# A trunk layer on one core: the first feed-forward regrouped from 6, 6, 6, 4 to 8, 8, 6 inner tiles, with the eights' down-projection in seven half products

## The chip, the core and the metric

The kernel runs on one core of a Trainium2 chip. TensorE (PE) multiplies, VectorE (DVE) and ScalarE (ACT) do element-wise work, GpSimd (POOL) and SyncE (SP) mostly start transfers. The metric is device microseconds of one execution; three runs of the kernel before gave 1647.42, 1647.49 and 1647.60 us, so the median is 1647.49 us. Lower is better.

## What is computed

One layer of a hybrid diffusion backbone on 128 context tokens and 512 latent tokens, 640 in all, each of width 1024, in fp32:

```python
mod = silu(cond) @ w_mod + b_mod                     # nine vectors: sh1, sc1, g1, shm, scm, gm, sh2, sc2, g2
h = modulate(rmsnorm(x, norm_g[0]), sh1, sc1)
x = x + 0.5 * g1 * swiglu(h, ffn1_w1, ffn1_w2)       # first feed-forward
h = modulate(rmsnorm(x, norm_g[1]), shm, scm)
y, C, n, m = mixer(h, ...)                           # mLSTM in two directions, short convolution, gates
x = x + gm * y
h = modulate(rmsnorm(x, norm_g[2]), sh2, sc2)
x = x + 0.5 * g2 * swiglu(h, ffn2_w1, ffn2_w2)       # second feed-forward
# swiglu(h, w1, w2): a, b = split(h @ w1); return (silu(a) * b) @ w2,  inner width 2816 = 22 tiles of 128
```

The context tokens have their own modulation vectors. A final RMSNorm and the mLSTM states are outputs too.

## The kernel before

The 640 tokens lie along the free axis in two halves of 320 columns, and every product is made of matmuls of 128x128 weights against 128x320 activations. To keep fp32 accuracy, each operand is split into a rounded high part (an ACT cast, line 75) and the remainder (a DVE subtraction, line 79), and one product is three matmuls (lines 288 to 290). The text calls these "main matmuls".

**Seven products for eight.** Two output tiles of a projection are made together as a "pair" (`pair_el`). Its weights and activations form 2x2 blocks (output tile by half of the contraction, half of the contraction by token half), and a Strassen-like scheme makes seven block products (`ORDER`: A11, S1, S2, A12, S3, S4, A22) where the plain way has eight. Each needs one weight block of 128x512 (some are sums of blocks, made by DVE at line 270, or, if the pair is "summed", by accumulating transfers on POOL's queue) and an activation operand, named 11, 21, 22, T1 to T4. With 8 tiles of contraction a pair has 7 x 4 x 3 = 84 main matmuls, where the plain way (`plain_el`) has 96.

**Feed-forward.** The 22 inner tiles go in groups: up-projection of a group, then its down-projection. The up-projection is in pairs (silu half and linear half of an inner tile), apart from the first tiles, which the "head" makes in the plain way while the modulated input is still being finished. A down-projection over 6 or 4 tiles is plain. In the first feed-forward the groups are 6, 6, 6, 4, and the residual X stays in SBUF, to which `add_x` (line 1017) adds. In the second they are 8, 8, 6: for a group of eight (`eights`) the inner activations are put into the seven operand forms (the sums by DVE), the down-projection is four pairs, the residual lies in DRAM (`xd`), results are added there by POOL's accumulating transfers (line 1030), and the input's forms T3 and T4 are parked in DRAM meanwhile (`h_away`, `h_back`). The last group, of six, is plain and ends in `halves_el`: three weight tiles for the left half of the tokens, then the same for the right half, with the next stage's norm (statistics at line 898, spreading at line 915, scaling, modulation and splitting of the next input) placed between the right half's products. In the group of four there are six such tiles of 12 matmuls.

**Modulation vectors.** The first gate (G1) is made on PE in eight units: 512 KB of w_mod each, two matmuls of 32x512 that occupy a quarter of the array's columns each (line 649). In the kernel before, POOL loads these into a pool of their own (`mg`), and two units are multiplied at one place. SHM, SCM and half of SH2 are made by DVE (`mod_dve`, lines 769 and 771: per unit four passes over 128x512), 20 units spread evenly over the feed-forward, and closed by matmuls with ones (line 780), SHM's two halves at one place and SCM's too.

**Order.** The order of the work on every engine is that in which the Python code emits it; nothing reorders it. Weights come through a ring of five 512 KB buffers (`wr`) on SP's queue, with splits made four operands ahead of the product that uses them.

Of the kernel before, what the change touches and what calls it, by code (L numbers as in the profile page):

```python
# [12 lines left out]
P = 128  # L13
# [31 lines left out]
def mixer_step(ctx: ExitStack, tc: tile.TileContext, x_prompt, x_sample, state_C, state_n, state_m,  # L45
# [503 lines left out]
    st = st_x.enter_context(pool("st"))  # L549
# [159 lines left out]
    def mod_own(ch):  # L709


        us, fs, tiles = [], [], {}
        for half in range(2):
            u, f = mod_half(ch, half, True)
            us += [(mod_load(ch, half, i, G), u[i][1]) for i in range(4)]
            fs.append(f)

        def load(*ii):
            for i in ii:
                tiles[i] = PO["mg"].tile([P, 1024], F32, name="mg", bufs=2)  # L720
                if i < 2:

                    G.tensor_copy(tiles[i][:, 0:1], modT[:, SH1, KT - 1, 0:1])
                us[i][0](tiles[i])

        def two(v, *more):
            def f():
                for i in (2 * v, 2 * v + 1):
                    us[i][1](tiles.pop(i))
                if v < 3:  # L730
                    load(2 * v + 2, 2 * v + 3)
                for m in more:
                    m()
            return f
        none = lambda: None
        return (lambda: load(0, 1),
                [two(0), none, two(1, fs[0][0]), fs[0][1], two(2, fs[0][2]), none, two(3, fs[1][0]), none], fs[1][1:])
# [68 lines left out]
    def with_units(main, units, spare=0):  # L806
# [4 lines left out]
        post = []  # L811
        for i, el in enumerate(main):
            el = dict(el, raws=list(el["raws"]), fill=list(el.get("fill", ())))
            now, post = post[:1], post[1:]
            while e < m and e * n < (i + 1) * m:
# [228 lines left out]
    def eights(w1, w2, g, f0, n_head, head, more, back):  # L1044
# [12 lines left out]
        def put_own(o, k, src):  # L1057
            UB[o][k] = hl = upair()
            split(src, *hl)
# [40 lines left out]
        for j in range(8):  # L1100
# [6 lines left out]
            if due:  # L1107
                pops = {1: (3, 2, 1), 2: (2, 2, 2), 3: (3, 2)}.get(due, (2, 8) if j < 5 else (8,))
                at = joined(at, {i + 1: [lambda n=n: relax_some(n)] for i, n in enumerate(pops)})
            if f0 + j < n_head:  # L1110
                head.extend(blocks_of(p))
            else:
                grp.append(pair_el(*p, at=joined(at, more.get(j, {})), spare_v=j in spare, calm=True,
                                   summed=j > (1 if f0 < n_head else 3)))
        w2s = []
        PO["x_end"] = []
        for m in range(0, KT, 2):
# [17 lines left out]
            elif m == KT - 2 and back:  # L1135
                at = {4: [lambda: h_back("T3")], 6: [lambda: h_back("T4")]}
            w2s.append(pair_el(w_load(w2, f0 * P, 8, m * P, D), w_load(w2, f0 * P, 8, (m + 1) * P, D), ev,
                               acts=UB, at=at, gated=rows_, spare_v=m == 0, summed=m == 0))
        return grp, w2s

    def ffn(w1, w2, g, lists, head_of, n_head, e1=None, groups=(6, 6, 6, 4), more={}):

        head, els, f0 = [], [], 0
        for gi, size in enumerate(groups):
            if size == 8:
                els.append(eights(w1, w2, g, f0, n_head, head, more.get(gi, {}), True))
                f0 += size
                continue
            U = {}
            grp = []  # L1150
            for j in range(size):
# [16 lines left out]
                else:  # L1168
                    grp.append(pair_el(*p, e1 if f0 == 0 else None, at=more.get(gi, {}).get(j)))
# [30 lines left out]
    PO["un"] = 12  # L1200
# [70 lines left out]
    def first_head(blocks):  # L1271
# [22 lines left out]
        def emit():  # L1294
# [74 lines left out]
            for f in lower(1, 6, 7):  # L1369
                f()  # L1370
            close_early()
# [53 lines left out]
    def close_early():  # L1425
        early_x.close()
        PO["hq"] = ctx.enter_context(pool("hq", side="right"))
# [40 lines left out]
    head, els = ffn(ffn1_w1, ffn1_w2, G1, after_lists(1, SHM), first_head, 3)  # L1468
    PO["ma_x"] = ExitStack()
    PO["mg_x"] = ExitStack()  # L1470

    def open_mg():
        PO["mg"] = PO["mg_x"].enter_context(pool("mg"))
    g_first, g_mid, g_last = mod_own(G1)
    prog += [head, step(open_mg), step(g_first)] + weave(els[0][0], [step(f) for f in g_mid])
    els[0][1][0] = dict(els[0][1][0], fill=[step(f) for f in g_last + [half_gate(G1)]])

# [3 lines left out]
    def open_ma():  # L1481
        PO["mg_x"].close()
        PO["ma"] = PO["ma_x"].enter_context(pool("ma"))

    def ma_wide():
        return [PO["ma"].tile([P, 512], F32, name="ma", bufs=4)]

    prog += [step(open_ma), step(gate_weights_)]
    main = []
# [751 lines left out]
```

## Time and profile before

| | us |
|---|---|
| median of 3 runs | 1647.49 |
| the profiled execution's own time | 1648.61 |
| its span, first to last instruction | 1646.8 |
| first feed-forward: head's end, then pairs up to the last plain product | 77.0 to 478.9 |
| second feed-forward: first pair to the last product | 1241.7 to 1646.8 |

The page lists each engine's busy share, groups of instructions, and the chain that ended last. A row of the stretches view reads: stretch, its length, then for each engine the busy time with the number of instructions, the granted TensorE clock, the share of the DMA engines that were busy, and GB/s. A row of the timeline reads: start, length, engine, line, operation, output<-inputs, shape and count; the length of a matmul contains its pipeline, so the distance of starts is what one costs.

### The profile page before, as it was taken

To read this page: it belongs to the slowest core of one execution; us is meant where nothing else is said; L and a number is where in the kernel's file an instruction comes from. 1 tells how busy PE (TensorE), PEld (TensorE's weight loads), DVE (VectorE), ACT (ScalarE), POOL (GpSimd) and SP (SyncE) were. 2 spreads that over 40 slices of the span, in tenths; PEclk is the share of its full clock that TensorE was granted. 3 is DMA by queue.
4 is the path that set the end of the run, shared out by engine and by line. 5 is a ranking of instruction groups with operands and counts; after the bars stand their busy time and mean duration, and the time that the engine had idled before them with its cause. 6 is when DMAs were issued, how large, how long until landed. Compare 5 with 4: busy or idle time off the path is not lost.

```text
span 1646.8 us, 29482 instructions
## 1 busy us (share of the span) xinstructions
PE 1628.1 (99%) x11093; PEld 1585.3 (96%) x11093; DVE 1284.7 (78%) x2714; ACT 837.8 (51%) x1841; POOL 251.9 (15%) x362
## 2 busy tenths in 40 slices
PE   7999999999999999999999999999999999999998
PEld 5989999999999999999999999999999999999997
DVE  6867887887878878787887788879778877786765
ACT  5542542542566656455562455642276665565543
POOL 2010000000031221121121222011133113113002
PEclk9999999999999999999999999999999999999999
DMA  9454343343353443342358333357468768468522
GB/s 321 117 164 120 99 127 114 110 119 100 103 172 101 109 106 87 81 114 70 96 165 270 109 90 90 91 167 222 136 177 179 156 134 197 105 134 199 167 81 65
DMA packets 302607, 220.88 MB, mean 134 GB/s; under 512 B 9844, under 2 KB 279547, under 8 KB 302465
## 3 DMA queue, kind: packets, MB, share of 16 engines
q1 hardware_dynamic: 269680, 161.50, 34.3%
q0 software_dynamic: 32752, 57.49, 14.7%
q8 instruction: 87, 1.43, 0.4%
q14 instruction: 56, 0.45, 0.1%
q10 hardware_dynamic: 32, 0.01, 0.0%
HBM read 193.18 MB, written 25.79 MB: 133 GB/s over the span
## 4 chain that ended last, share of the span: by engine, by line
PE 89%; DVE 4%; ACT 3%; DMA 2%; issue 1%; SPq 1%; POOL 0%; ACTq 0%; DVEq 0%; POOLq 0%
PE ps L288 27%; PE ps L289 27%; PE ps L290 27%; PE ax L1780 2%; PE ax L1811 2%; DMA wr<-in_ffn_w_dram 1%; PE ax L1783 1%; DVE wl L79 1%; PE ax L1757 1%; ACT Uh L931 1%; ACT wh L75 1%; SPq L627 0%; DMA wl<-in_x_sample_dram 0%; DVE Uh L923 0%; PE ax L780 0%
## 5 line engine op out<-in xcount | busy, mean ns | idle before, releaser
L79 DVE TENSOR_TENSOR wl<-wr,wh 128x512 fp32r<-128x512 f32 (+1 forms) x401 | 272.9, 692 | 86.3 <-ACT wh L75 83.9
L75 ACT CAST wh<-wr 128x512 fp32r<-128x512 f32 (+1 forms) x403 | 235.8, 598 | 91.1 <-PE ps L289 71.3
L79 DVE TENSOR_TENSOR wl<-ws,wh 128x512 fp32r<-128x512 f32 x300 | 207.5, 692 | 56.2 <-ACT wh L75 55.6
L75 ACT CAST wh<-ws 128x512 fp32r<-128x512 f32 x300 | 183.7, 620 | 96.9 <-DVE ws L270 68.9
L288 PE MATMUL ps<-Uh,wh 128*128 128x320 f32 x576 | 179.6, 312 | 0.0
L289 PE MATMUL ps<-Ul,wh 128*128 128x320 f32 x576 | 177.9, 309 | 0.0
L290 PE MATMUL ps<-Uh,wl 128*128 128x320 f32 x576 | 177.7, 308 | 0.0
L288 PE MATMUL ps<-HT4h,wh 128*128 128x320 f32 x408 | 128.4, 315 | 0.0
L289 PE MATMUL ps<-HT4l,wh 128*128 128x320 f32 x408 | 126.4, 310 | 0.6 <-DVE HT4l L79 0.5
L290 PE MATMUL ps<-HT4h,wl 128*128 128x320 f32 x408 | 126.1, 309 | 0.0
L288 PE MATMUL ps<-H11h,wh 128*128 128x320 f32 x376 | 118.8, 316 | 0.5 <-ACT H11h L75 0.5
L288 PE MATMUL ps<-H21h,wh 128*128 128x320 f32 x376 | 117.7, 313 | 0.0
L289 PE MATMUL ps<-H11l,wh 128*128 128x320 f32 x376 | 116.5, 310 | 0.3
L290 PE MATMUL ps<-H21h,wl 128*128 128x320 f32 x376 | 116.3, 309 | 0.0
L290 PE MATMUL ps<-H11h,wl 128*128 128x320 f32 x376 | 116.1, 309 | 0.0
L289 PE MATMUL ps<-H21l,wh 128*128 128x320 f32 x376 | 116.1, 309 | 0.0
L288 PE MATMUL ps<-HT3h,wh 128*128 128x320 f32 x356 | 111.8, 314 | 0.1
L289 PE MATMUL ps<-HT3l,wh 128*128 128x320 f32 x356 | 110.0, 309 | 0.0
L290 PE MATMUL ps<-HT3h,wl 128*128 128x320 f32 x356 | 110.0, 309 | 0.0
L288 PEld LDWEIGHTS ps<-Uh,wh 128*128 128x128 f32 x576 | 108.1, 188 | 1.2 <-issue 0.8
L289 PEld LDWEIGHTS ps<-Ul,wh 128*128 128x128 f32 x576 | 108.2, 188 | 0.4 <-DVE Ul L79 0.4
L290 PEld LDWEIGHTS ps<-Uh,wl 128*128 128x128 f32 x576 | 108.1, 188 | 0.0
(483 smaller groups left out, 4722.9 us busy)
## 6 DMA issues: line engine op xcount, KB each, us to landing
wr<-in_ffn_w_dram SPq DMA_DIRECT2D x90, 512.0 KB, 4.8
wr<-in_w_in_dram SPq DMA_DIRECT2D x72, 512.0 KB, 3.9
wr<-in_w_mod_dram SPq DMA_DIRECT2D x51, 512.0 KB, 3.9
wr<-in_ffn_w_dram SPq DMA_DIRECT2D x32, 384.0 KB, 3.3
xd<-x POOLq DMA_DIRECT2D x32, 320.0 KB, 6.0
wr<-in_ffn_w_dram SPq DMA_DIRECT2D x36, 256.0 KB, 4.3
early<-in_w_mod_dram SPq DMA_DIRECT2D x13, 512.0 KB, 9.2
wr<-in_ffn_w_dram POOLq DMA_DIRECT2D x24, 256.0 KB, 5.0
```

Source lines behind the costliest of these rows:

```text
L75: A.copy(hi, raw)
L79: V.tensor_sub(lo, raw, f32(hi))
L288: PE.matmul(ps, hi[:, ws], ah, start=start, stop=False, skip_group_check=True)
L289: PE.matmul(ps, hi[:, ws], al, start=False, stop=False, skip_group_check=True)
L290: PE.matmul(ps, lo[:, ws], ah, start=False, stop=stop, skip_group_check=True)
L931: A.activation(t[:, a:b], t[:, a:b], AF.Identity, scale=sc_, bias=bi_)
L1757: PE.matmul(p[:, :P], S["k", dt][:, sl], S["q", dt][:, sl], start=(dt == 0), stop=(dt == 1))
L1780: PE.matmul(p2[:, :DH + 1], S["q", dt][:, sl], S["C"][d][:, dt, :], start=(dt == 0), stop=(dt == 1))
L1783: PE.matmul(p1[:, :DH + 1], S["p", ch][:, d, :], PO["vt"][:, ch, :], start=True, stop=True)
L1811: PE.matmul(p[:, :DH + 1], kw[:, dt * P:(dt + 1) * P], PO["vt"][:, ch, :], start=True, stop=True)
```

## The change

The first feed-forward takes the groups 8, 8, 6. Its two eights go through `eights`, as in the second: seven operand forms, four pairs each for the down-projection, X in DRAM, T3 and T4 of the input parked. X is written to `xd` inside the head (`spill_x`, after a POOL copy that waits for SH1's last piece) and read back in the third group's up-projection. The first gate's eight units now come through the weight ring, two to each of the first four pairs of the up-projection, and each is multiplied at a place of its own. `mod_dve`'s 20 units go to places from a table, and each vector half is closed on its own (no `joint`). Which pairs are summed is now an argument; in the first feed-forward, where none was, it is the fourth to the last pair of each eight, the first two pairs of each eight's down-projection, and the last four pairs of the third group. The pool for inner activations has 15 buffers of each kind instead of 12, and the sixteenth operand pair borrows the tile `sqacc`.

```diff
-    def mod_own(ch):
-        ...
+    def with_own(pairs, ch, *last):
+        us, fs = zip(*[mod_half(ch, half, True) for half in range(2)])
+        out = []
+        for p, el in enumerate(pairs):
+            el = dict(el, raws=list(el["raws"]))
+            fill = []
+            for i in (2 * p, 2 * p + 1) if p < 4 else ():
+                load, unit_ = us[i // 4][i % 4]
+                at_ = len(el["raws"])
+                el["raws"].append(load)
+                def go(unit_=unit_, at_=at_, el=el):
+                    unit_(raw(el["base"] + at_))
+                    rdone.add(el["base"] + at_)
+                    load_more()
+                fill += [step(go), step(lambda: None)]
...
+            if places:
+                el["fill"], now = el["fill"] + now, []
+            while e < m and (e < due[i] if places else e * n < (i + 1) * m):
...
         def put_own(o, k, src):
-            UB[o][k] = hl = upair()
+            if PO["un"] < 16 and (o, k) == ("11", 0):
+                t = tp.tile([P, T], F32R, name="sqacc")
+                UB[o][k] = hl = t[:, hsl(0)], t[:, hsl(1)]
+            else:
+                UB[o][k] = hl = upair()
...
-    PO["un"] = 12
+    PO["un"] = 15
...
+            G.tensor_copy(tp.tile([P, 3], F32, name="rstd", bufs=2)[:, 0:1], modT[:, SH1, KT - 1, 0:1])
+            spill_x()
             close_early()
...
-    head, els = ffn(ffn1_w1, ffn1_w2, G1, after_lists(1, SHM), first_head, 3)
+    head, els = ffn(ffn1_w1, ffn1_w2, G1, after_lists(1, SHM), first_head, 3, (8, 8, 6), more_of(4),
+                    ({4, 5, 6, 7}, {4, 5, 6, 7}, {2, 3, 4, 5}), {0, 2}, {0: (2, 2, 1), 1: (2, 2, 1), 2: (3, 2)})
...
-    prog += with_units(main + w2s[:-1], mod_dve(SHM, (0, 1), ma_wide, True) + mod_dve(SCM, (0, 1), ma_wide, True) +
-                   mod_dve(SH2, (0,), ma_wide), 2)
+    prog += [head] + with_own(els[0][0], G1, half_gate(G1))
+    els[0][1][0] = dict(els[0][1][0], first=[open_ma, gate_weights_])
+    w2s = els[2][1]
+    prog += with_units(els[0][1] + els[1][0] + els[1][1] + els[2][0] + w2s[:-1],
+                       mod_dve(SHM, (0, 1), ma_wide) + mod_dve(SCM, (0, 1), ma_wide) + mod_dve(SH2, (0,), ma_wide),
+                       places=[0, 2, 1, 0] + [1, 0, 0, 0, 1, 0, 0, 0] + [0, 2, 1, 1] + [1] * 6 + [1] * 5)
```

Over the whole program PE's list holds 9972 main matmuls before and 9876 after; DVE's holds 2716 instructions before and 2732 after, ACT's 1815 and 1927, POOL's 367 and 470.

PE in the first pair of the first up-projection, before: two gate units (four matmuls from `mg`) behind the product S2.

```order
L290 MATMUL ps<-HT2h,wl 128x320
L649 MATMUL ax<-mg,cm 32x512 x4
L288 MATMUL ps<-H21h,wh 128x320
L289 MATMUL ps<-H21l,wh 128x320
L290 MATMUL ps<-H21h,wl 128x320
```

And now: one unit (two matmuls from the ring), one product earlier; seven more such places follow.

```order
L290 MATMUL ps<-HT1h,wl 128x320
L649 MATMUL ax<-wr,cm 32x512 x2
L288 MATMUL ps<-HT2h,wh 128x320
L289 MATMUL ps<-HT2l,wh 128x320
L290 MATMUL ps<-HT2h,wl 128x320
```

The gate has eight places on PE instead of four, each with half of the matmuls.

DVE at the end of the first feed-forward, before, from the first scaled piece of the mixer's input on (`Ul`, `Uh` are the scaled X, `wl` a weight's remainder; line 1017 adds a product to X):

```order
L923 TENSOR_TENSOR Ul<-x,ax 128x320
L923 TENSOR_TENSOR Uh<-x,ax 128x320
L923 TENSOR_TENSOR Ul<-x,ax 128x320
L1017 SCALAR_TENSOR_TENSOR x<-ps,modT,x 128x320
L79 TENSOR_TENSOR wl<-wr,wh 128x512
L1017 SCALAR_TENSOR_TENSOR x<-ps,modT,x 128x320
L79 TENSOR_TENSOR wl<-wr,wh 128x512
L923 TENSOR_TENSOR Uh<-x,ax 128x320
L923 TENSOR_TENSOR Ul<-x,ax 128x320
L1017 SCALAR_TENSOR_TENSOR x<-ps,modT,x 128x320
L79 TENSOR_TENSOR wl<-wr,wh 128x512
L923 TENSOR_TENSOR Uh<-x,ax 128x320
```

And now, from the same place to the first input tile's remainder (`H11l`):

```order
L922 TENSOR_TENSOR Ul<-x,ax 128x320
L922 TENSOR_TENSOR Uh<-x,ax 128x320
L922 TENSOR_TENSOR Ul<-x,ax 128x320
L1016 SCALAR_TENSOR_TENSOR x<-ps,modT,x 128x320
L79 TENSOR_TENSOR wl<-wr,wh 128x512 x2
L922 TENSOR_TENSOR Uh<-x,ax 128x320
L922 TENSOR_TENSOR Ul<-x,ax 128x320
L922 TENSOR_TENSOR Uh<-x,ax 128x320
L922 TENSOR_TENSOR Ul<-x,ax 128x320
L932 TENSOR_SCALAR Ul<-Ul,gcol,modT 128x128
L932 TENSOR_SCALAR Ul<-Ul,gcol,modT 128x192
L79 TENSOR_TENSOR H11l<-Ul,H11h 128x320
```

Before, three additions and three weight splits stand in this stretch, and one more scaling, two modulations and the remainder follow it; now the remainder stands behind one addition and two weight splits. On PE, 9 main matmuls instead of 12 stand between the left half's end and the statistics, 9 instead of 12 between these and the spreading, and 36 instead of 48 from there to the next head's gate unit.

POOL behind the head, before: the two loads of gate weights, each behind a copy that waits for SH1.

```order
L923 TENSOR_TENSOR Uh<-x,t_373 128x320
L923 TENSOR_TENSOR Ul<-x,t_373 128x320
L723 COPY mg<-modT 128x1
L620 DMA mg<-in_w_mod_dram 128x2x512
L723 COPY mg<-modT 128x1
L620 DMA mg<-in_w_mod_dram 128x2x512 x7
L1533 MEMSET gw 128x256
```

And now: X's eight tiles, four accumulating weight loads, then the parking of T3 and T4.

```order
L922 TENSOR_TENSOR Ul<-x,t_373 128x320
L1375 COPY rstd<-modT 128x1
L1551 DMA xd<-x 128x640 x8
L235 DMA wr<-in_ffn_w_dram 128x4x128 x4
L1035 DMA hd<-HT3h 128x320
L1035 DMA hd<-HT3l 128x320
```

The gate's loads went over to SP's queue, and POOL's queue carries X, the weight sums and the parked tiles in their place.

More of the change, by code (lines that the diff above doesn't have):

```diff
@@ L804, in mod_dve, with with_units @@
         return units
[L806 removed]
+    def with_units(main, units, spare=0, places=None):
         out = []
@@ L811, in with_units @@
         post = []
+        due = [sum(places[:i + 1]) for i in range(len(main))] if places else None
         for i, el in enumerate(main):
```

86 lines of the change are left out of this document (31 added, 55 removed).

## The prediction

> **What bounds the kernel now.** I read the page's busy shares and the chain first, then stretches cut at the stage boundaries, then single places in PE's timeline.
>
> ```profile
> span 1646.8 us, 29482 instructions
> PE 1628.1 (99%) x11093; PEld 1585.3 (96%) x11093; DVE 1284.7 (78%) x2714; ACT 837.8 (51%) x1841; POOL 251.9 (15%) x362
> PE 89%; DVE 4%; ACT 3%; DMA 2%; issue 1%; SPq 1%; POOL 0%; ACTq 0%; DVEq 0%; POOLq 0%
> ```
>
> PE is busy all the way and is 89% of the chain that ended last: the time is PE's list of matmuls plus the few places where it does not run at its own pace. So I price the change in matmuls first, then in what interrupts them. The stretches, in order a plain down-projection of six tiles and six up pairs in the first feed-forward, then the two eights' down-projections of the second, which already has the form that the first is to get:
>
> ```profile
> 120.33:163.01 42.68, 42.68 (x295) 42.67 (x293) 31.98 (x67) 10.40 (x21) 0.00 (x0) 1.00 0.43 124
> 163.01:236.84 73.83, 73.83 (x506) 73.83 (x505) 59.97 (x108) 37.93 (x80) 0.00 (x0) 1.00 0.37 108
> 1316.09:1366.45 50.36, 50.03 (x339) 49.26 (x337) 37.44 (x67) 30.77 (x70) 9.57 (x15) 1.00 0.68 151
> 1464.99:1515.29 50.30, 49.97 (x339) 49.27 (x337) 37.37 (x66) 30.77 (x70) 9.58 (x15) 1.00 0.69 154
> ```
>
> Six pairs are 504 main matmuls (the count has two that only reach into the stretch): 73.83 / 504 = 0.1465 us each. By that the plain group's 288 take 42.19, and the 42.68 is that plus one group of transposes, so nothing waits there. The clock column is 1.00 throughout.
>
> **The change, part by part.** *Fewer products.* The 22 inner tiles' down-projection was 22 x 8 x 2 x 3 = 1056 main matmuls; two eights in four pairs of 84 and six plain tiles make 672 + 288 = 960. The order's totals fall by the same 96. 96 x 0.1465 = **-14.06 us**, all on the path.
>
> *Hand-over into the eights' pairs.* 336 main matmuls would take 49.22; the two rows above show 50.36 and 50.30, so 1.14 and 1.08 are lost where the first pair waits for its last operand forms. The plain group lost nothing. I take **+2.22**; the same code runs there, so the bounds are 1.5 (first pair already rid of its DVE sums) and 3.
>
> *The first gate's units.* Two kinds of group stand in the first up-projection:
>
> ```profile
> 82.80 0.31 PE L290 MATMUL ps<-HT2h,wl 128*128 128x320 f32 x1
> 83.04 1.07 PE L649 MATMUL ax<-mg,cm 128*32 128x512 f32 x8
> 84.04 0.41 PE L288 MATMUL ps<-H21h,wh 128*128 128x320 f32 x1
> ...
> 91.03 0.31 PE L290 MATMUL ps<-HT4h,wl 128*128 128x320 f32 x1
> 91.27 1.56 PE L649 MATMUL ax<-mg,cm 128*32 128x512 f32 x8
> 92.77 0.42 PE L288 MATMUL ps<-H11h,wh 128*128 128x320 f32 x1
> ```
>
> From the last main matmul to the first after it 1.24 us pass, or 1.74 where the second unit came after the first instead of beside it; the main matmul behind it is 0.10 longer (0.41 for 0.31). Less one normal step a group costs 1.24 - 0.15 + 0.10 = 1.19, the late one 1.69; of the four groups one was late, so 3 x 1.19 + 1.69 = 5.26. In the first kind the two units occupy different columns at one time, so a unit by itself should take as long as two: eight places at 1.19 are 9.52, **+4.26**. The lower bound follows from the second kind: an additional unit adds 0.50 when the array is already in that form; if entry and exit cost a lone unit nothing, 8 x 0.50 is 1.26 less than before. I stay by 1.19, since each of the eight has main matmuls on both sides.
>
> [...]
>
> *SHM and SCM closed half by half.*
>
> ```profile
> 247.25 0.31 PE L290 MATMUL ps<-Uh,wl 128*128 128x320 f32 x1
> 247.49 1.07 PE L780 MATMUL ax<-ma,ones 128*32 128x256 f32 x16
> 248.49 0.41 PE L288 MATMUL ps<-Uh,wh 128*128 128x320 f32 x1
> ...
> 447.77 0.31 PE L290 MATMUL ps<-HT4h,wl 128*128 128x320 f32 x1
> 448.01 0.64 PE L780 MATMUL ax<-ma,ones 128*32 128x256 f32 x8
> 448.57 0.41 PE L288 MATMUL ps<-Uh,wh 128*128 128x320 f32 x1
> ```
>
> Priced the same way, a joint group is 1.24 - 0.15 + 0.10 = 1.19 and a single 0.80 - 0.15 + 0.10 = 0.75: before 2 x 1.19 + 0.75 = 3.13, after 5 x 0.75 = 3.75, **+0.62**. Transposes are as many as before.
>
> *The end of the feed-forward.* The last group is now six tiles deep, so the right half's products behind which the mixer's norm hides are 54 matmuls, not 72.
>
> ```profile
> 467.98 0.49 DVE L880 TENSOR_TENSOR sqacc<-sqacc,t 128x320 f32<-128x320 f32 x1 [0.61 <-ACT t L876]
> 468.11 0.31 PE L290 MATMUL ps<-Uh,wl 128*128 128x320 f32 x1
> 468.53 0.83 PE L898 MATMUL ax<-ones,sqacc 128*128 128x2 f32 x6
> 469.91 0.68 DVE L908 TENSOR_SCALAR dg<-ident,rstd 128x128 f32<-128x128 f32 x3
> 471.07 0.83 PE L915 MATMUL ax<-dg,ones 128*128 128x128 f32 x6
> 479.67 0.48 DVE L79 TENSOR_TENSOR H11l<-Ul,H11h 128x320 fp32r<-128x320 f32 x1
> 480.21 0.41 PE L289 MATMUL ps<-H11l,wh 128*128 128x320 f32 x1
> PE ax L898 <- DVE sqacc L880: 0.5, 1, 0.5
> ```
>
> The statistics already wait for `sqacc` (ready at 468.47) behind 12 matmuls; behind 9 they wait 3 x 0.1465 = 0.44 longer. The spreading needs the diagonals (ready at 470.59) 2.06 after the statistics began; 9 matmuls fill 1.32 of it and the statistics about 0.7 (their 0.83 less what overlaps): about 0.1. The first H11l came just in time, 8.6 us after the spreading; PE's 12 fewer matmuls shorten that by 1.76, and DVE's list loses two additions and a split there (0.45 + 0.45 + 0.65 = 1.55, from the 0.49 and 0.68 kinds in these rows): no difference. The second statistics, which wait 0.5 now, stand behind two more weight splits, 0 to 1.3; I take 0.6. Together **+1.1**, bounds 0 and 2.5.
>
> *The start.* Behind the head PE waited once, for an ACT copy queued behind six splits of inner activations that a step between head and pair had flushed:
>
> ```profile
> PE ps L288 <- ACT ps L332: 0.4, 1, 0.4
> ```
>
> That step is gone and the splits are spread: **-0.3** (0 to -0.5). X's spill takes the place of the gate's first loads on POOL:
>
> ```profile
> L723 POOL COPY mg<-modT x2: 187/350/512, 45.4 to 46.7; 128x1 f32<-128x1 f32 x2
> L1541 POOL DMA_DIRECT2D xd<-x x16: 539/540/600, 482.5 to 1214.2; - x16
> DMA to landing us min/median/max: 3.2/6.0/9.9
> 55.89 0.31 PE L288 MATMUL ps<-H11h,wh 128*128 128x320 f32 x1
> ```
>
> Issued from 45.5 at 0.54 each, the first tile's is down by 51.5, 55.4 at worst; the first write over it (the first inner tile's silu in `eights`) comes when the head's right half ends, at 55.9. Nothing, but without much room.
>
> *DVE's and the ring's crowding.* The eights need more DVE work (sums of operands, 28 splits for 16), the summed pairs less. The rows are an eight's second and third down pair of the second feed-forward, one up pair, and the passes of one modulation unit:
>
> ```profile
> 1329.51:1341.82 12.31, 12.31 (x86) 12.31 (x85) 9.61 (x17) 7.07 (x16) 2.26 (x3) 1.00 0.64 139
> 1341.82:1354.13 12.31, 12.31 (x86) 12.31 (x85) 7.99 (x14) 6.77 (x16) 1.72 (x3) 1.00 0.70 140
> 1428.07:1440.37 12.30, 12.30 (x86) 12.30 (x85) 9.78 (x20) 6.98 (x16) 1.58 (x2) 1.00 0.64 128
> L771 DVE SCALAR_TENSOR_TENSOR ma<-wr,cm,ma x70: 743/748/755, 125.6 to 438.1; 128x512 f32<-128x512 f32 x70
> L270 DVE TENSOR_TENSOR ws<-wr x130: 671/684/1170, 63.5 to 1577.0; 128x512 f32<-128x512 f32 x130
> ```
>
> A unit is 4 x 0.75 = 3.0 us. The second down pair of each eight gets two and saves two sums: 9.61 + 6.0 - 1.37 = 14.2 us of DVE in 12.31 of PE; the third 7.99 + 3.0 = 11.0, the fourth about as much or 8. So a backlog of 1.9 arises and melts in the two pairs behind it. Splits run four operands, about 7 us, ahead, but a read of S3's accumulator must end within one product (1.76), and there a backlog reaches PE. I take half of one of the two: **+1.0**; 0 below, 5 above (next part).
>
> Sum: -14.06 + 2.22 + 4.26 + 0.62 + 1.1 - 0.3 + 1.0 = -5.16. From the profiled execution's 1648.61 (1.8 around its span) that is 1643.45, and from the median, 1.12 lower, **1642.3 us**.
>
> **The rivals.** *Crowding eats it.* If no backlog is absorbed, the two second down pairs cost 1.9 each, the fifth up pair of the second eight 9.78 + 3.0 - 12.30 = 0.5, and the last group's five plain products, each with a unit, (31.98 - 4 x 3.0) / 8 + 3.0 = 5.5 against 5.28, 1.1 in all: 5.4 in place of 1.0, 1646.7. For it: PE's dependence within one product; against: the plain stretch at 163.01 has pairs with a unit at over 11 of 12.3 and loses nothing.
>
> *The ring starves the first up-projection, slower.* A pair there takes four of the five buffers, and the sums' buffer comes free only with the gate unit in the pair's last product, 10.5 us in. The base load, the accumulating one and the split must follow before the second product two pairs on, at 26.4.
>
> ```profile
> 1253.98:1266.75 12.77, 12.77 (x90) 12.76 (x89) 9.48 (x20) 7.41 (x17) 10.27 (x18) 1.00 1.22 281
> DMA to landing us min/median/max: 4.4/5.2/6.0
> wr<-in_w_mod_dram SPq DMA_DIRECT2D x51, 512.0 KB, 3.9
> ```
>
> That is 10.5 + 3.9 + 5.2 + 1.3 = 20.9, 5.5 to spare. The second pair also parks 2.6 MB; its twin in the second feed-forward (first row) moved 3.6 MB, this one gets 1 MB more. If loads and additions took twice as long from there, 30.0, three pairs would stall 3.6 each: 1642.3 + 10.8 = 1653. It decides from 5.5 us of additional latency. Against it: the twin pair kept its pace (12.77 with 0.4 of transposes).
>
> [...]
>
> *Switching is cheaper than priced.* If a lone unit costs about its 0.50, the gate term falls by 5.5; with the crowding at 0 the time is 1636 to 1638. For it only that 0.50.
>
> That the change does not do what it says is excluded by the order's 96 fewer main matmuls.
>
> **How the numbers follow.** Forecast 0.55, crowding 0.22, cheaper switching 0.16, starving ring 0.07. The forecast's own terms reach from 1640 to 1644.5. Two tenths (3.3 us, 1644.2) is about what a measurement can tell from no change. Cheaper switching and nearly all of the forecast lie below it, and a little of the crowding: faster 0.74; the rest of these two, same 0.19; the ring, slower 0.07. The range takes in most of both faster cases and of the crowding: 1638.0 to 1646.8.
>
> **What would show it.** Right: the two new down-projections at about 50.4 in place of 56, eight lone gate groups at 1.24 from main to main, five closings at 0.80, a statistics wait near 0.7 at the end of the feed-forward, no difference behind the mixer's start. Wrong: gate groups of under 1 us; waits on `wl` or on S3's accumulator in down pairs with two units; waits for `wr` in the first up-projection; the silu behind the head waiting for X's spill.

## The result: slower by 1.3%, and the profile after

The kernel after took 1669.87 us in the median of four runs (1663.24 to 1674.53), the kernel before 1647.53 in four beside them (1647.42 to 1647.60): 1.0133 times as long, with a 95% interval of 1.0098 to 1.0167. Forecast were 1642.3 and a range up to 1646.8. The profiled execution is the one of 1670.03; the forecast for it is 1648.61 - 5.16 = 1643.45, so 26.6 us are to be found.

The page of the kernel after, its busy times and its chain:

```profile
span 1667.9 us, 29682 instructions
PE 1628.7 (98%) x10997; PEld 1577.0 (95%) x10997; DVE 1301.8 (78%) x2730; ACT 881.7 (53%) x1953; POOL 337.7 (20%) x465
PE 82%; DVE 8%; DMA 4%; ACT 4%; issue 2%; POOL 0%; SPq 0%; ACTq 0%; DVEq 0%; POOLq 0%
```

PE's busy time is what it was (1628.1), with 96 main matmuls fewer, and PE's share of the chain fell from 89% to 82%: DVE has 8% for 4%, DMA 4% for 2%. So PE now waits, and part of its work has become slower. The stretches of the kernel after, cut at the first main matmul of each stage (up-projection and down-projection of the first, second and third group), say where. Columns as before; PEclk and the DMA share are the last but two and one.

```profile
76.00:148.75 72.75, 72.18 (x462) 63.72 (x461) 53.57 (x108) 39.83 (x90) 19.57 (x25) 1.00 0.84 203
148.75:199.97 51.22, 50.13 (x338) 49.28 (x337) 43.45 (x77) 30.55 (x69) 13.47 (x21) 1.00 0.85 197
199.97:299.54 99.57, 99.57 (x684) 98.85 (x683) 80.01 (x151) 54.78 (x119) 19.77 (x22) 1.00 0.69 153
299.54:351.79 52.25, 51.13 (x346) 49.44 (x345) 44.48 (x78) 31.01 (x70) 11.56 (x16) 1.00 0.83 194
351.79:444.55 92.76, 79.53 (x519) 77.87 (x517) 61.92 (x114) 39.39 (x85) 20.80 (x26) 0.94 0.78 194
444.55:500.96 56.41, 50.50 (x338) 46.74 (x336) 41.42 (x90) 19.29 (x44) 8.13 (x9) 0.94 0.39 110
```

The number to read is the length less the stage's main matmuls at 0.1465 each, "lost" below. Worked out in the same way for both kernels, from the starts of the main matmuls in the traces:

| stage | before: main matmuls, length, lost | after: main matmuls, length, lost |
|---|---|---|
| first group, up | 252, 43.31, 6.40 | 420, 72.75, 11.22 |
| first group, down | 288, 42.68, 0.49 | 336, 51.22, 2.00 |
| second group, up | 504, 73.83, 0.00 | 672, 99.57, 1.13 |
| second group, down | 288, 43.88, 1.69 | 336, 52.24, 3.02 |
| third group, up | 504, 73.99, 0.16 | 504, 92.76, 18.92 |
| third group, down | 288, 43.87, 1.68 | 288, 56.41, 14.22 |
| fourth group, up and down | 528, 81.28, 3.93 | - |
| all | 2652, lost 14.35 | 2556, lost 50.5 |

From the mixer's first product to the end both kernels take 1167.0 us. The 96 matmuls are gone and gave their 14.06. What ate them stands in two rows: the third group's up-projection lost 18.9 where 0.2 was lost before, and the last down-projection 14.2 where the forecast has about 7 (the 5.6 that the third group's down-projection and the fourth group lost before, and at most 1.7 from its terms for closings and end). Those are some 19 and 7 of the 26.6. They are also the only two rows with a granted clock of 0.94.

What PE waited for in the kernel after, in the last two stages (who waited, for what; us in total, times, the longest):

```profile
PE ps L288 <- DVE t L360: 13.2, 4, 6.1
PE ax L776 <- DVE ma L767: 4.5, 3, 3.2
PE ax L784 <- ACT t L779: 0.8, 1, 0.8
PE ax L897 <- DVE sqacc L879: 0.6, 1, 0.6
```

Line 360 is the DVE addition that reads the accumulator of product S3 and so frees it for a later one; line 767 is a modulation unit's pass (771 before), 776 and 784 its closing.

### Reading the first: a weight that came late

The second of the four waits for line 360, the kernel after, followed back engine by engine (start, length, what; in brackets the idle time before it and what ended it). PE:

```profile
375.94 0.31 PE L290 MATMUL ps<-H22h,wl 128*128 128x320 f32 x1
381.01 0.42 PE L288 MATMUL ps<-HT4h,wh 128*128 128x320 f32 x1 [4.76 <-DVE t L360]
```

DVE, whose addition stands behind weight splits that wait for ACT's cast:

```profile
371.07 0.75 DVE L767 SCALAR_TENSOR_TENSOR ma<-wr,cm,ma 128x512 f32<-128x512 f32 x1
378.66 0.69 DVE L79 TENSOR_TENSOR wl<-wr,wh 128x512 fp32r<-128x512 f32 x1 [6.85 <-ACT wh L75]
...
380.48 0.48 DVE L360 TENSOR_TENSOR t<-ps,t 128x320 f32<-128x320 f32 x1
```

ACT, whose cast waits for the weight to land:

```profile
378.01 0.62 ACT L75 CAST wh<-wr 128x512 fp32r<-128x512 f32 x1 [6.57 <-DMA wr<-in_ffn_w_dram]
```

SP, which issued that load, and POOL's transfers just ahead of it:

```profile
367.84 0.37 SPq L218 DMA_DIRECT2D wr<-in_ffn_w_dram  x1
```

```profile
365.60 2.62 POOL L235 DMA_DIRECT2D wr<-in_ffn_w_dram  x2 [9.13 <-DVE t L367]
367.14 2.87 POOL L1029 DMA_DIRECT2D xd<-x  x2
```

So the addition on which PE waited had all of its inputs; it stood in DVE's row behind the split of a weight that took 10.1 us from issue (367.84) to landing (377.94). The load itself went out late, because SP was standing before it. The other three waits for line 360 end in the same way, behind loads that took 7.3, 11.2 and 6.9 us; the one of 11.2, in front of the longest wait, went out at 386.35 among X's eight tiles on their way back from DRAM. SP's waits of the kernel after, between 340 and 440:

```profile
SPq L218 <- DVE ma L767: 54.4, 6, 11.3
```

Six loads, about one a pair and the first of them still in the second group, wait for the last pass of a modulation unit. In the third group every pair carries a unit, its buffer of the ring of five comes free only with that last pass, and the next pair's plain load needs it. And the load was slow; this is what moved beside it:

```profile
367.00:378.00 11.00, 9.25 (x64) 8.98 (x62) 4.82 (x11) 2.67 (x6) 3.00 (x3) 1.00 1.04 187
```

The DMA engines are busy all the time (1.04) at only 187 GB/s, with POOL's accumulating transfers to weight sums and to X under way. In the prediction's row at 1253.98 they carried 281 at 1.22.

### Reading the second: half the clock after a wait

Apart from the last 10 us of the execution, where both kernels have one (from 1643.16 before, from 1661.38 after), three stretches of the kernel after have a granted clock of 0.50:

```profile
381.40:384.80 3.40, 3.40 (x15) 3.40 (x14) 2.52 (x6) 2.15 (x5) 3.21 (x6) 0.50 0.39 49
398.40:405.20 6.80, 3.98 (x15) 3.98 (x16) 5.92 (x12) 3.46 (x8) 2.64 (x2) 0.50 0.58 107
477.00:483.70 6.70, 5.08 (x22) 4.17 (x21) 3.23 (x11) 2.02 (x5) 1.68 (x2) 0.50 0.53 145
```

They follow the waits of 4.76, 6.10 and 3.24 us. In them the main matmuls start 0.267 apart in place of 0.1465:

```profile
381.95 0.47 PE L289 MATMUL ps<-HT4l,wh 128*128 128x320 f32 x1
382.22 0.47 PE L290 MATMUL ps<-HT4h,wl 128*128 128x320 f32 x1
```

Thirteen or so in each, 0.12 more apiece, make about 1.5 us for each window, on top of the wait. The up-projection's 18.9 are 13.2 of waits, about 0.3 more for each to get going again, and two windows; of the other 1.5, a closing and two pairs of transposes make about 1.2.

### Reading the third: DVE's chain in the last group

In the last down-projection each of the first five plain products (36 main matmuls, 5.28 us) carries one unit. DVE, kernel after, in one product's length and the start of the next:

```profile
468.11 2.97 DVE L767 SCALAR_TENSOR_TENSOR ma<-wr,cm,ma 128x512 f32<-128x512 f32 x4
471.00 1.13 DVE L1016 SCALAR_TENSOR_TENSOR x<-ps,modT,x 128x128 f32<-128x128 f32 x3
473.18 1.72 DVE L79 TENSOR_TENSOR wl<-wr,wh 128x512 fp32r<-128x512 f32 x2 [1.05 <-ACT wh L75]
474.82 2.97 DVE L767 SCALAR_TENSOR_TENSOR ma<-wr,cm,ma 128x512 f32<-128x512 f32 x4
```

The period is 474.82 - 468.11 = 6.71: about 5.6 of work and 1.05 in which DVE waits for ACT's casts. These stand on ACT behind squares that wait for DVE's own additions:

```profile
471.70 0.93 ACT L875 ACTIVATE t<-x 128x320 f32<-128x320 f32 x2 [5.00 <-DVE x L1016]
```

The units of the five products start at 449.72, 455.74, 461.29, 468.11 and 474.82, so the four periods are 6.0, 5.6, 6.8 and 6.7. DVE falls behind PE, by 1.4 and more in each of the last two, and the closing of SH2's half, which needs the last pass, stops PE:

```profile
472.85 0.31 PE L290 MATMUL ps<-Uh,wl 128*128 128x320 f32 x1
476.40 0.63 PE L776 MATMUL ax<-ma,ones 128*32 128x256 f32 x4 [3.24 <-DVE ma L767]
```

From 472.85 to the next main matmul, at 480.05, 7.05 are lost; an earlier closing, with its wait of 0.45, cost 1.8 more, and the half clock about 1.5. The change also gives the passes two buffers (`ma`) where they had four; that took no part, since DVE never stood ahead of a unit's first passes (line 765).

### The profile page after: what moved, and what is told of

The parts are those of the page before. It is cut to its first block, busy times and chain, and to the rows that moved or that the text cites. A ratio compares the mean times of both kernels' runs of the same rounds, so it can differ in the third digit from the quotient of the medians.

```text
span 1667.9 us, 29682 instructions
## 1 busy us (share of the span) xinstructions
PE 1628.7 (98%) x10997; PEld 1577.0 (95%) x10997; DVE 1301.8 (78%) x2730; ACT 881.7 (53%) x1953; POOL 337.7 (20%) x465
## 4 chain that ended last, share of the span: by engine, by line
PE 82%; DVE 8%; DMA 4%; ACT 4%; issue 2%; POOL 0%; SPq 0%; ACTq 0%; DVEq 0%; POOLq 0%
PE ps L288 25%; PE ps L289 24%; PE ps L290 24%; DMA wr<-in_ffn_w_dram 4%; DVE wl L79 2%; PE ax L1789 2%; PE ax L1820 2%; DVE ma L767 1%; PE ax L1792 1%; ACT wh L75 1%; DVE ws L270 1%; PE ax L1766 1%; ACT Uh L930 0%; DVE x L1016 0%; DVE HT4l L79 0%
## 5 line engine op out<-in xcount | busy, mean ns | idle before, releaser
L288 PE MATMUL ps<-HT4h,wh 128*128 128x320 f32 x440 | 140.7, 320 | 15.9 <-DVE t L360 13.2
L235 POOL DMA_DIRECT2D wr<-in_ffn_w_dram x56 | 72.7, 1469 | 329.8 <-DMA wr<-in_ffn_w_dram 167.2
L289 PE MATMUL ps<-HT4l,wh 128*128 128x320 f32 x440 | 137.7, 313 | 0.6 <-DVE HT4l L79 0.5
L288 PE MATMUL ps<-Uh,wh 128*128 128x320 f32 x440 | 138.2, 314 | 0.0
L290 PE MATMUL ps<-HT4h,wl 128*128 128x320 f32 x440 | 137.2, 312 | 0.0
L289 PE MATMUL ps<-Ul,wh 128*128 128x320 f32 x440 | 136.7, 311 | 0.0
L290 PE MATMUL ps<-Uh,wl 128*128 128x320 f32 x440 | 136.3, 310 | 0.0
L288 PE MATMUL ps<-HT3h,wh 128*128 128x320 f32 x388 | 121.8, 314 | 0.2
L288 PE MATMUL ps<-H22h,wh 128*128 128x320 f32 x344 | 107.7, 313 | 0.0
L289 PE MATMUL ps<-H22l,wh 128*128 128x320 f32 x344 | 106.4, 309 | 0.4
```

The costliest lines, as they stand in the source:

```text
L235: queue.dma_start(t[:, 512 * o:512 * o + 512].rearrange("p (k n) -> p k n", k=4), dap(w, (row0 + 512 * half) * ncol + col0, [[ncol, P], [P ...
L288: PE.matmul(ps, hi[:, ws], ah, start=start, stop=False, skip_group_check=True)
L289: PE.matmul(ps, hi[:, ws], al, start=False, stop=False, skip_group_check=True)
L290: PE.matmul(ps, lo[:, ws], ah, start=False, stop=stop, skip_group_check=True)
```

## The experiments

The readings leave open which of three things in the third group's up-projection makes the loads late: the modulation units that hold the ring's buffers (T1), X being read back from DRAM there in one go (T2), or the summed pairs' accumulating weight loads (T3); they all stand in the same pairs. Four variants of the kernel after take one apart each. In the same job the kernel before took 1648.09. Each variant ran once, and the kernel after's own runs spread over 11 us, so a difference of a few us between single times shows little; the waits in the traces say more. The diffs are against the kernel after unless it says otherwise.

**No units in the third up-projection.** SH2's half is left out, one unit goes to the second up-projection, and one stays in the stage instead of six.

```diff
+    G.memset(modT[:, SH2, 0:4], 0.0)
...
-                       mod_dve(SHM, (0, 1), ma_wide) + mod_dve(SCM, (0, 1), ma_wide) + mod_dve(SH2, (0,), ma_wide),
-                       places=[0, 2, 1, 0] + [1, 0, 0, 0, 1, 0, 0, 0] + [0, 2, 1, 1] + [1] * 6 + [1] * 5)
+                       mod_dve(SHM, (0, 1), ma_wide) + mod_dve(SCM, (0, 1), ma_wide),
+                       places=[0, 2, 1, 0] + [1, 0, 1, 0, 1, 0, 0, 0] + [0, 2, 1, 1] + [1, 0, 0, 0, 0, 0] + [1] * 5)
```

> Five of the six modulation units of the third group's pairs are taken away (one stays in its first pair; two more alternate pairs of the second group get one, and the first half of SH2, four units and their closing, is left out and set to zero: about 1 us of matmuls less). Theory 1, the ring: a unit keeps its ring buffer until its last DVE pass at the pair's end, so the load five buffers on starts late, ACT stands at its cast and PE waits for the eviction behind it. Expected: the waits of PE on line 360 (13.2 us in the changed kernel) and two of the three half-clock windows go, the third group's pairs take 74 to 76 us instead of 93, about 1651 us. Theory 2, transfers: X's read back and the parked tiles crowd the DMA engines and POOL's queue: waits stay, above 1660. Theory 3, the summed loads' chain is too long: waits stay, above 1660.

1651.06 us, and the stage takes 74.0 us, as T1 had it. PE's only listed wait from 345 to 430 lies just ahead of the stage, at 350:

```profile
PE ps L288 <- DVE x L325: 0.5, 1, 0.5
```

The stage lost 0.16, as before the change, though the sums and X's read-back are still there, and no half-clock window is left in it. Slow loads alone do not stop PE: the one issued at 383.61, while X's tiles were coming back, took 8.4 us here. The last down-projection, which kept its units, lost 13.64. The units are necessary for the loss.

**No summed pairs in the third group.**

```diff
-                    ({4, 5, 6, 7}, {4, 5, 6, 7}, {2, 3, 4, 5}), {0, 2}, {0: (2, 2, 1), 1: (2, 2, 1), 2: (3, 2)})
+                    ({4, 5, 6, 7}, {4, 5, 6, 7}, ()), {0, 2}, {0: (2, 2, 1), 1: (2, 2, 1), 2: (3, 2)})
```

> The third group's pairs load both weight tiles plainly and DVE makes the sums; units and X's transfers stay. Theory 3, the summed chain: waits go, about 1652 us. Theory 1, the ring: an unsummed pair with a unit takes three of the five buffers as well, so loads stay late: waits of at least 6 us remain, 1660 or more. Theory 2: waits remain, less traffic on POOL, about 1660.

1660.04 us. PE still waits 5.0 us for line 360 in the stage, in two waits (T1 had at least 6), and the stage lost 9.4. SP still waited 52.5 us for the units, so the sums are not what makes the loads late, as T1 has it; but half of the loss went with them, which T1 alone does not explain. That they make the late loads slow is not shown: without them POOL comes to X's additions and read-back earlier (355.5 to 368), and beside these the loads issued at 356.35 and 367.52 took 17.3 and 9.0 us; the next two of their kind, with none of POOL's transfers beside them, took 3.8 and 3.6.

**X read back three pairs later**, in the group's last pair.

```diff
-                2: {0: {4: [x_end, lambda: PO.pop("xs")]}, 2: {1: [x_whole]}}}
+                2: {0: {4: [x_end, lambda: PO.pop("xs")]}, (5 if p == 4 else 2): {1: [x_whole]}}}
```

> X's eight tiles are read back in the third group's sixth pair instead of its third. Theory 2, transfers: the loads that took 8 to 11 us to land take 4 to 6 and the second wait (6.1 us) is gone, about 1655 us. Theory 1, the ring: the first wait (4.8 us, ahead of that read) is unchanged and the others of the same order: 1663 or more. Theory 3: as theory 1.

1659.78 us, between the two theories' times and a miss for both. The wait at 376 is gone, which T1 alone did not foresee. The longest, of 6.1 at 395, is gone too, as T2 had it, and one of 4.7 stands at 412, behind the place to which the read-back went; the load issued there at 404.73 took 9.4 us.

```profile
PE ps L288 <- DVE t L360: 4.7, 1, 4.7
```

The wait that went shows how fine the margin is. In this run SP's load and POOL's additions to X stand so, SP first:

```profile
365.67 0.37 SPq L218 DMA_DIRECT2D wr<-in_ffn_w_dram  x1
```

```profile
364.40 2.63 POOL L235 DMA_DIRECT2D wr<-in_ffn_w_dram  x2 [8.94 <-DVE ws L270]
365.95 2.87 POOL L1029 DMA_DIRECT2D xd<-x  x2
```

The load went out 0.3 ahead of the second group's last additions to X and landed in 5.2 us; in the kernel after it went out 0.7 behind them and took 10.1. Fractions of a microsecond decide, which would also explain the spread of the kernel after's runs (1663 to 1675); that part is argued, not shown.

**Units earlier in their pair.** Steps are spread evenly over a pair's products. Four empty ones at the end move a unit's passes forward, and with them the release of its buffer.

```diff
             if places:
                 el["fill"], now = el["fill"] + now, []
...
+            if places and el["fill"]:
+                el["fill"] += [step(lambda: None)] * 4
```

> Where a pair or product has modulation passes by the table, four empty fills are put behind them, so that the passes stand in the first half of the pair; nothing else moves. Theory 1, the ring: the unit's buffer is freed about 6 us sooner in each pair, and the waits on line 360 fall below 4 us in all: about 1653 us. Theories 2 and 3: the waits stay, above 1662.

1653.31 us, as T1 had it. Nothing is left out, and SP's wait for the units fell from 54.4 us to

```profile
SPq L218 <- DVE ma L767: 10.3, 5, 2.6
```

The stage lost 5.6: one wait of 2.55 us, a half-clock window behind it (the main matmuls start 0.26 to 0.27 apart from 402.24 on; the clock is 0.98 over the 78.50 us from 351.50), and small ones. T1 stands as the condition. X's transfers (T2) stand beside the slowest loads in these runs; the part of the sums (T3) was not separated from them.

**No units in the last group** (SH2's half left out, one more unit in the second up-projection; the third up-projection keeps its six). Theory A is the third reading: DVE's chain in the last group by itself makes that stage's loss, whatever happens ahead of it. In this job the kernel before took 1647.88 in the median of 15 runs.

```diff
+    G.memset(modT[:, SH2, 0:4], 0.0)
...
-                       mod_dve(SHM, (0, 1), ma_wide) + mod_dve(SCM, (0, 1), ma_wide) + mod_dve(SH2, (0,), ma_wide),
-                       places=[0, 2, 1, 0] + [1, 0, 0, 0, 1, 0, 0, 0] + [0, 2, 1, 1] + [1] * 6 + [1] * 5)
+                       mod_dve(SHM, (0, 1), ma_wide) + mod_dve(SCM, (0, 1), ma_wide),
+                       places=[0, 2, 1, 0] + [1, 0, 1, 0, 1, 0, 0, 0] + [0, 2, 1, 1] + [1] * 6 + [0] * 5)
```

> The last group's five plain products lose their modulation units (one goes to the second group; the first half of SH2, four units, is left out and set to zero); the third group's pairs keep theirs, one each. Theory A, the last group is bound by DVE: a unit's four passes beside an element's casts, additions and squares take 6.7 us of DVE where PE takes 5.3, so the closing matmuls wait 3.2 + 0.8 + 0.8 us and the clock halves for 6.8 us. Expected: these waits and that half-clock window go, the waits on line 360 in the third group stay, about 8 us less than the changed kernel's usual 1670 (1659 to 1665). Rival, the waits there are only the delay that came out of the third group: they stay, above 1666.

1657.54 us, a little below the range that was given. The waits for closings are gone from the last group, the third up-projection still lost 15.1. PE's waits in the up-projection:

```profile
PE ps L288 <- DVE t L360: 9.0, 3, 4.4
```

The last down-projection lost 4.3 for 14.2, where the closing of SH2's half, left out, is part of the difference. In the run without units in the third up-projection next to nothing (0.16) was lost just ahead of this stage, and it still lost 13.64. So the rival is out, and the two losses are separate.

**Idle time alone, in the kernel before.** Is it the wait that halves the clock? At the start of the first, second and third down-projection PE gets two small matmuls with a chain of 3, 20 or 9 DVE passes between them, and nothing else changes. The diff is against the kernel before.

```diff
+    def idle(n):
+        def f():
+            p = aux()
+            PE.matmul(p[:, :P], ones, ones, start=True, stop=True)
+            t = t3()
+            V.tensor_copy(t[:, :P], p[:, :P])
+            for _ in range(n):
+                V.tensor_scalar(t[:, :P], t[:, :P], 1.0, None, op0=OP.mult)
+            PE.matmul(p[:, :2], t[:, :P], ones[:, :2], start=True, stop=True, skip_group_check=True)
+        return f
+    for i, n in ((0, 3), (1, 20), (2, 9)):
+        els[i][1][0] = dict(els[i][1][0], first=[idle(n)])
```

> The kernel before, with three artificial waits of PE at the starts of the first, second and third plain down-projection: a chain of 3, 20 and 9 DVE passes over 128x128 between two small matmuls. Theory, the clock follows PE's idle time: waits of about 1 us cost just themselves, waits of 2.5 us or more are followed by a half-clock window of 3.4 or 6.8 us, which costs half of it again. Rival, the windows in the changed kernel have another cause: no window here, and the time grows by the three waits alone.

1673.78 us, 25.9 more than the kernel before. The waits were 3.53, 7.96 and 5.09 us, and each has its window, of 6.8, 10.2 and 6.8 us; the wait of about 1 us that the expectation speaks of did not come about, since the chain of 3 passes gave the 3.53:

```profile
PE ax L1497 <- DVE t L1496: 16.6, 3, 8.0
```

```profile
122.60:129.40 6.80, 6.47 (x25) 6.43 (x26) 3.92 (x11) 0.00 (x0) 0.00 (x0) 0.50 0.23 77
245.50:255.70 10.20, 4.43 (x17) 4.43 (x18) 8.79 (x28) 0.58 (x2) 0.00 (x0) 0.50 0.23 73
375.20:382.00 6.80, 5.03 (x19) 5.03 (x20) 5.28 (x13) 0.00 (x0) 0.00 (x0) 0.50 0.27 82
```

Idle time alone does it. The price is smaller than I had expected, because a longer window begins while PE still waits (it is busy for 4.43 of the 10.20 us): 13 to 16 main matmuls run at half speed in each, 1.6 to 1.9 us. Of the 25.9, 16.6 are the waits and about 5.3 the clock; the remaining 4.0 I put down to the six small matmuls with their way in and out.

**Both causes removed.** Units early in their pair; X read back two tiles a pair from the third pair on; the units of the last group's fourth and fifth product moved to the second up-projection, and one unit of the second group's down-projection a pair later. The second of the two kernels has this alone, the first also puts the gate's two units of a pair at one place again, as in the kernel before.

```diff
-                2: {0: {4: [x_end, lambda: PO.pop("xs")]}, 2: {1: [x_whole]}}}
+                2: {0: {4: [x_end, lambda: PO.pop("xs")]}, **({2 + i: {1: [lambda i=i: [x_in(m) for m in (2 * i, 2 * i + 1)]]}
+                                                           for i in range(4)} if p == 4 else {2: {1: [x_whole]}})}}
...
+            if places and el["fill"]:
+                el["fill"] += [step(lambda: None)] * 4
...
-                       places=[0, 2, 1, 0] + [1, 0, 0, 0, 1, 0, 0, 0] + [0, 2, 1, 1] + [1] * 6 + [1] * 5)
+                       places=[0, 2, 1, 0] + [1, 0, 1, 0, 1, 0, 1, 0] + [0, 1, 2, 1] + [1] * 6 + [1, 1, 1, 0, 0])
```

and for the first kernel, in `with_own`:

```diff
-                fill += [step(go), step(lambda: None)]
+                gos.append(go)
+            if gos:
+                both = step(lambda gos=tuple(gos): [g() for g in gos])
+                fill = [step(lambda: None), both, step(lambda: None), step(lambda: None)]
             if p == 2:
-                fill[1] = step(fs[0][0])
-                fill[3:] = [step(f) for f in fs[0][1:]]
+                fill = [step(fs[0][0]), both] + [step(f) for f in fs[0][1:]]
```

> Full result. Four things on top of the changed kernel: passes of a unit in the first half of its pair (as in the run before), units moved so that the last group has three, in its first three products, X's eight tiles read back two to a pair, and the gate's two units of a pair multiplied at one place. If the two causes (late ring buffers, DVE in the last group) are the whole difference to my prediction, this comes to 1642.3 - 4.3 (four gate groups fewer) = 1638, no half-clock window before the end. If something third costs, it stays above 1643.

> The same without the joint gate units: eight lone groups on PE. If a lone group costs 1.19 us as I priced it, 4.3 us slower than the run with four (about 1642); if entering and leaving the small form is cheap, the same time within 1 us.

With joint gate units 1641.9 us (six runs, 1641.55 to 1644.5), 0.9968 of the kernel before (0.9955 to 0.998): 0.3% faster than it, and faster than the kernel after. With single ones 1645.94 (ten runs), 0.9988 (0.9978 to 0.9997). Up-projection of the first group, and the last two stages, of the kernel with joint units:

```profile
76.52:144.44 67.92, 67.70 (x462) 63.09 (x461) 53.78 (x108) 39.63 (x90) 19.52 (x25) 1.00 0.90 216
...
348.94:424.59 75.65, 75.65 (x524) 74.39 (x523) 62.45 (x114) 39.27 (x85) 20.96 (x26) 1.00 0.97 244
424.59:472.60 48.01, 46.77 (x331) 44.63 (x329) 36.47 (x80) 19.11 (x43) 8.19 (x9) 1.00 0.33 98
```

and the first, with single ones:

```profile
76.27:148.19 71.92, 71.92 (x462) 63.69 (x461) 53.65 (x108) 39.99 (x90) 19.67 (x25) 1.00 0.85 206
```

The clock is 1.00 in all of these; the last two stages lost 1.8 and 5.8. X's tiles and the sums still move in the stage that had 194 GB/s, in less time and so at 244, and PE does not stand. 1641.9 is above the 1638 that I had expected of it. Of the waits that are left in the feed-forward none is over 0.9 us; the two kinds that make up most of them are for DVE operations that free an accumulator:

```profile
PE ps L288 <- DVE x L325: 1.6, 3, 0.7
PE ps L288 <- DVE t L360: 1.4, 2, 0.9
```

## Why the prediction was wrong, step by step

*Fewer products, -14.06.* Right: 2556 main matmuls for 2652, and the remaining ones kept 0.1465 wherever the clock was full and nothing was waited for.

*Hand-over, +2.22.* Too high: the first pair of each eight's down-projection, where the hand-over lies, lost 0.35 and 0.65. The two stages lost 2.00 and 3.02 all the same. The rest is a closing in the second (0.8) and the two middle pairs, where PE waited four times, 2.1 us in all, for the addition that frees S3's accumulator (line 325):

```profile
PE ps L288 <- DVE x L325: 2.1, 4, 0.8
```

These middle pairs, with two units and one, lost 3.2 together. That is the crowding for which the sum looked, and for which it had 1.0; it is one of the signs that the prediction named for being wrong. Together the two terms came to 4.2 for 3.2.

*Gate units alone, +4.26.* Right. The group before and behind a single unit, kernel after:

```profile
79.38 0.30 PE L290 MATMUL ps<-HT1h,wl 128*128 128x320 f32 x1
79.61 1.05 PE L649 MATMUL ax<-wr,cm 128*32 128x512 f32 x4
80.59 0.42 PE L288 MATMUL ps<-HT2h,wh 128*128 128x320 f32 x1
```

1.21 from main to main where 1.24 was said, and the two last kernels, which differ in nothing else, lost 10.39 and 6.39 there: 4.0 us for four more groups. That settles the rival of cheaper switching: it is out, and a group more cost 1.0 us here.

*Closings, +0.62, and the start, -0.3.* The first pair came 1.0 earlier, not 0.3 (at 76.00 for 77.01); the cause of that stays open. Three of the five closings did not wait and took 0.80 to 0.81 from main to main, as forecast; what failed is that the other two had to wait.

*The end, +1.1.* Partly: the first statistics wait 0.6, near the 0.7 of the forecast, but the second ones wait 0.6 for 0.5 before, not 0.6 more, and from the mixer's first product on nothing was lost.

*Crowding, +1.0 from "half of one of the two" down pairs: the step that failed, in two ways.*

First, place. The sum looked for crowding in the down-projections, and the up-projection of the third group, with a unit in each of its six pairs, got no term. It rested on the plain stretch at 163.01, where "pairs with a unit at over 11 of 12.3" lost nothing. But in that stretch the pairs are not summed, X is not moved and nothing accumulates (108 GB/s, against 194), and about half of the six pairs have a unit. SP waited for units there too, 26.4 us in three waits, but the plain weight loads landed within 3.4 to 6.6 us, so one that went out late still landed in time. The rival of the starving ring had the mechanism, a buffer that comes free late and a load that is slow beside accumulating transfers, and a point from which it decides, 5.5 us of additional latency. The load that was followed above took 10.1 us, where the row in the prediction has 3.9: 6.2 more, past that point. I applied it to the first up-projection alone, where PE lost 0.6 to a wait, and gave it 0.07. What I should have done is to go through every stage in which a buffer is held to a pair's end and ask what else moves at that time. The runs without units in that stage (lost 0.16) and with early units (5.6) show it.

Second, size. "The last group's five plain products" were put at 5.5 against 5.28, 1.1 in all, and only in the rival. DVE's work is indeed 5.6 a product, but its period rose to 6.7: it waits 1.05 for ACT's casts, which wait for DVE's additions. A busy sum is the lower end of an engine's period where two engines wait for each other in turn. Without the units there the stage lost 4.3 instead of 14.2.

*No term at all: the clock.* The row said 1.00 throughout before, and I took it for a constant. It was 1.00 while PE stood nowhere in this feed-forward for more than 0.5 us; in the kernel after three waits of over 3 us brought three windows at half speed, about 4.6 us together. Any stall's price was therefore too low in the rivals too.

With both causes away the kernel with single gate units gains 1.94, not 5.16. What is still missing, 3.2, is not itemised to the end. In its trace PE waits 4.7 us in all between 76 and 478, never over 0.92 at a time, and 2.8 of it for DVE operations that free an accumulator (lines 325 and 360); for hand-over and crowding together the sum had 3.2. The second group's up-projection, with two units more in its pairs, lost 3.2 (1.1 in the kernel after), of which 1.4 are such waits and 0.8 is a closing.

## What to carry to other kernels

Where a ring's buffers are lent to a side job, look at what frees them and at what moves beside the next load in that very stage; a stage that bears the same job without that traffic proves nothing for it. Take an engine's busy time as its period only if it never waits for an engine that waits for it. A stall of PE with a half-clock window behind it, of which 2.55 us was the shortest that was read here, cost by estimate 1.5 to 1.9 us above its own length (13 to 16 main matmuls at 0.267 for 0.1465), and belongs into a sum at that price.

## What the hardware showed that I had not expected

*The granted clock inside a dense kernel.* In the kernel after, behind the first 10 us, single waits of up to 1.42 us (at 430.37) left the clock at 1.00. Longer ones were followed by windows at 0.50: there 3.4 us after the wait of 4.76, 6.8 after the one of 6.10, and 6.8 after the closings' three waits in a row (3.24, 0.82, 0.80); in the kernel before with idle time 6.8 after 3.53, 10.2 after 7.96 and 6.8 after 5.09; in the run with early units the wait of 2.55 was enough. The windows' lengths are one, two or three times 3.4, and which of these does not follow from the wait's length alone: 3.53 brought 6.8, and 4.76 brought 3.4.

In the kernel after the windows begin at 381.38, 398.45 and 476.95, five and 23 steps of 3.413 us apart; the three in the kernel before with idle time, at 122.6, 245.5 and 375.2, lie 36 and 38 such steps apart. With the kernel after's execution laid out in these steps, PE idled 3.05, 3.33 and 2.86 us in the steps just ahead of the three windows. It idled 1.72 in the one from 374.56 on, with the first part of the wait of 4.76, and 1.20 in the one with the wait of 1.42, and the clock was 1.00 behind both; no other step between the head's end and the last 10 us at full clock has more than 0.94. At half clock, the steps with 2.77 and 1.62 us of idle time were followed by another at 0.50, and the windows ended behind steps with 0.00. (This is idle time as the profile shows it. The window in the last 10 us came behind a step with 0.87.) Where between these values the clock changes was not measured.

*Accumulating transfers.* In the stretch at 367 the DMA engines were fully busy (1.04) at 187 GB/s, and a 512 KB load took 10.1 us from issue to landing; the same load, issued 1.0 us sooner relative to two additions to X in the run with X read back later, took 5.2. Which share of this is the additions' and which the weight sums' was not measured apart; in the run without summed pairs in this group a load among X's transfers, with no weight sums under way, took 9.0.
